# Two blocks of a transformer on one core: the score matmuls of two heads issued as one unit, in the two halves of the array's rows

## The chip, the cores and the metric

The kernel runs on one core of a Trainium2 chip. The metric is the device time of one execution in microseconds (us). Before the change it is 2282.53 us, the median of three runs (2281.49 to 2285.62).

## The reference, cut to what matters

The program has two blocks on 256 tokens of width 1024: a first block of two layers (mixers with three branches, a dense feed-forward, a mixture of experts), and a second block with two attention layers, called fox and dsw. Three pieces of it are attentions with heads of 64 channels, and they alone are touched. In short:

```python
# A: differential attention, one branch of the mixer, in both layers; 4 heads, two maps (m) each
s = einsum('bhmqd,bhmkd->bhmqk', qb, k)
s = where(mask, s - slopes * dist, -inf)
p = softmax(s); a = p[:, :, 0] - lam * p[:, :, 1]

# fox: 16 heads, causal, with a running sum c of log gates
s = einsum('bqhd,bkhd->bhqk', qi, k) * scale + ci[..., None] - c_k[:, :, None, :]
o = softmax(where(mask, s, -inf)) @ v

# dsw: 16 heads, three groups of dilated windows, softmax joined over the groups
s = einsum('znqhd,znkhd->znhqk', qb, band(kb)) * scale
```

All of it is float32, and the score products are float32 matmuls with 64 rows of contraction (the channels of a head).

## The kernel before, in words

Every engine call goes through a recorder (class `Recorder`, line 57). `add` (line 85) notes an operation with its engine, its tiles, its predecessors and an estimated cost, and `flush` (line 151) puts all operations of the program in order: a list scheduler that lets five engines run on its cost table, gives each engine the ready operation of highest priority, and hands out tiles of a tag strictly in the order in which they were asked for. The resulting order is then issued, and each engine runs its part in that order. All recorded instructions therefore carry one line number, L88, that of the closure in `add`.

PSUM has 8 banks: 3 with the tag `pa` (projections), 4 with `pb` (attention and other small work), 1 with `pt`. A bank counts as one region, whatever part of it is used.

Weights arrive as float32 (`raw`, on the queue of SP), ACT rounds them to a high part (`wh`), DVE subtracts to get the low part (`wl`), and TensorE multiplies in three passes with the activations' own two parts (`hh`, `hl`). This is most of TensorE's work. The attentions are woven between such projections.

An attention works on pairs of heads. The channels of the pair's first head lie in partitions 0 to 63 of the transposed queries and keys, those of the second in 64 to 127. For each head `e` of the pair a unit goes as follows: scores into one `pb` bank `p`; DVE masks them and finds the maxima; ACT takes exponentials into a tile `E2`; TensorE transposes the result into another `pb` bank; ACT copies that to SBUF; TensorE multiplies with the values into a third `pb` bank `o`, which the pair's units share.

- `a_heads` (line 1190): per pair 2 heads by 2 query blocks `b`; in each unit two maps `m`, each with a score matmul and then a bf16 matmul that adds the bias (identity times `biasA`).
- `fox`, its inner `attend` (line 1572): per pair 2 units; in each 4 bf16 matmuls that add the gates' sums, then score matmuls of 128 and of 256 columns. `attend(0)` is woven with projections, `attend(1)` with the first part of the output projection (`out_early`).
- `dsw`, its inner `attend` (line 1771): per pair 2 heads by 2 query blocks; in each unit three score matmuls, of 256, 128 and 128 columns, one per group. The four `attend` are woven with the next quarter's projections, the last one with `out_early`.

A float32 matmul leaves two records of a weight load and two of a matmul in the trace, of the same shape. There are 160 score matmuls: 32 in A, 32 in fox, 96 in dsw.

Of the kernel before, what the change touches and what calls it, by code (L numbers as in the profile page):

```python
# [4 lines left out]

# [1 line left out]

# [34 lines left out]
SWITCH, WAIT, URGENT, LOOK, RELEASE, TICK = 3000.0, 100.0, 20.0, 300.0, 1000.0, 10240 / 3  # L42
# [6 lines left out]


class Op:
    __slots__ = ("eng", "fn", "tiles", "dur", "table", "preds", "succs", "left", "ready", "prio", "bytes", "cols", "bias", "wait", "at", "name")


ENGINES = {"tensor": "PE", "vector": "DVE", "scalar": "ACT", "gpsimd": "POOL", "sync": "SP"}
# [3 lines left out]
class Recorder:  # L59
# [7 lines left out]
            setattr(s, name, Queue(s, name))  # L67

    def reset(s):
        s.ops, s.hist, s.bias, s.wait = [], {}, 0.0, WAIT  # L70

    def region(s, ap):

# [8 lines left out]
        ext = sum(abs(k) * (c - 1) for k, c in list(ap.ap)[1:]) + 1  # L82
        return t, p, p + n, f * size, (f + ext) * size

    def add(s, engine, method, args, kw):
        op = Op()
        op.eng, op.bias, op.wait = ENGINES[engine], s.bias, s.wait
        op.fn = lambda: getattr(getattr(s.nc, engine), method)(*args, **kw)  # L88
        aps = [x for x in args[1:] if hasattr(x, "tensor")] + [
            x for k, x in kw.items() if hasattr(x, "tensor") and k != "accum_out"]  # L90
        outs = [args[0]] + ([kw["accum_out"]] if kw.get("accum_out") is not None else [])
        s.cost(op, method, args, kw, outs[0], aps)
        op.name = method, outs[0].tensor.name, [z.tensor.name for z in aps]
# [3 lines left out]
        i = len(s.ops)  # L97
        preds = set()
        hit = lambda a, b: a[1] < b[2] and b[1] < a[2] and a[3] < b[4] and b[3] < a[4]
        for r in rd:  # L100
            ws, rs = s.hist.setdefault(r[0], ([], []))
            preds.update(j for q, j in ws if hit(q, r))
            if s.tag_of[r[0]] in BANKS:
                preds.update(j for q, j in rs if s.ops[j].eng != op.eng)
            rs.append((r, i))
        for r in wr:
            ws, rs = s.hist.setdefault(r[0], ([], []))
            preds.update(j for q, j in ws if hit(q, r))
            preds.update(j for q, j in rs if j != i and hit(q, r))
            inside = lambda q: r[1] <= q[1] and q[2] <= r[2] and r[3] <= q[3] and q[4] <= r[4]  # L110
            ws[:] = [z for z in ws if not inside(z[0])] + [(r, i)]
            rs[:] = [z for z in rs if z[1] == i or not inside(z[0])]
        op.preds = preds
        s.ops.append(op)

# [213 lines left out]
class Net:  # L329
# [860 lines left out]
    def a_heads(s, hp, qT, kT, va, neglam, sub, ya):  # L1190
        nc = s.nc
        o = s.ps("pb", (128, 4, 128))
        for e in range(2):
            h = 2 * hp + e
            ro = slice(e * 64, e * 64 + 64)
            for b in range(2):
                nk = 128 * (b + 1)
                p = s.ps("pb", (128, 2, 256))
                for m in range(2):
                    nc.tensor.matmul(p[:, m, 0:nk], qT[ro, 2 * m + hp, b * 128:b * 128 + 128],  # L1200
                                     kT[ro, 2 * m + hp, 0:nk], start=True, stop=False)
                    nc.tensor.matmul(p[:, m, 0:nk], s.identb, s.biasA[:, h, 256 - nk:256], start=False, stop=True)
                mx, sm = s.t([128, 2], "sa"), s.t([128, 2], "sa")
                nc.vector.tensor_reduce(mx, p[:, :, 0:nk], AX.X, ALU.max, negate=True)
                ex = s.t([128, 2, 256], "E2")
# [11 lines left out]
                at = s.t([128, 256], "E2")  # L1217
# [287 lines left out]
    def fox(s):  # L1505
# [66 lines left out]
        def attend(hf, T, v):  # L1572
            zh, zl = zs[hf]
            for pr in range(4):
                o = s.ps("pb", (128, 2, 2, 65))
                for e in range(2):
                    h = hf * 8 + pr * 2 + e
                    ro = slice(64 * e, 64 * e + 64)
                    q, k = T[0][ro, pr], T[1][ro, pr]
                    p = s.ps("pb", (128, 384))  # L1580
# [150 lines left out]
    def dsw(s):  # L1731
# [39 lines left out]
        def attend(qt, T, V):  # L1771

            z = zs[qt]
            for pr in range(2):
                o = s.ps("pb", (128, 2, 2, 65))
                for e in range(2):
                    ro = slice(64 * e, 64 * e + 64)
                    q, k = [T[g][ro, pr] for g in range(3)], [T[g][ro, 2 + pr] for g in range(3)]
                    vh = lambda g, kb: V[g][:, kb, pr * 2 + e]
                    for b in range(2):  # L1780
                        sl = slice(b * 128, b * 128 + 128)
# [8 lines left out]
                        for i, v in enumerate((vh(0, 0), vh(0, 1), vh(1, b), vh(2, b))):  # L1790
# [99 lines left out]
```

## Time and profile before

| what | us |
|---|---|
| median of three runs | 2282.53 |
| profiled execution, its own time | 2282.9 |
| its span, first to last instruction | 2280.9 |
| PE busy (matmul) | 2187.4 |
| DVE busy | 1733.8 |
| ACT busy | 1370.1 |
| attention A, layer 0 (stretch of the span) | 240 to 292 |
| attention A, layer 1 | 768 to 822 |
| attention fox | 1786 to 1896 |
| attention dsw | 1990 to 2264 |

PE is the matmuls of TensorE, PEld its weight loads, which overlap matmuls; DVE is VectorE, ACT ScalarE, POOL GpSimd, SP SyncE. Matmuls are pipelined, so a record is longer than the time from one start to the next: costs are read from start to start. A name such as `pb<-F,F` is the output's tile and the operands' tiles, with buffer numbers left out: `F`, `M`, `macc`, `g` hold transposed queries and keys in the attentions, `P` values, `E` softmax results, `T` and `G` other small tiles; a single operand name means that both operands lie in one tile. "64\*128" are the rows and columns of the array that a matmul uses.

### The profile page before, as it was taken

What the parts mean: (1) busy time and instruction counts of PE and PEld (TensorE: products, weight loads), DVE (VectorE), ACT (ScalarE), POOL (GpSimd) and SP (SyncE); (2) the same over time, 40 slices, a digit from 0 to 9 for tenths busy, and PEclk for the clock granted to TensorE, in tenths of its full rate; (3) what the DMA queues carried; (4) which work ended last, traced back from release to release, by engine and by line L of the source; (5) the groups of instructions that cost most, each with busy time, mean ns of one, the idle gap of its engine ahead of it and who ended that gap; (6) DMA issues with size and microseconds to landing.
All of it is one profiled execution on the core that took longest, in us unless ns stands there. A gap on an engine that the chain in (4) does not pass through costs nothing. (4 is left out here: it accounts for less than half of the span.)

```text
span 2280.9 us, 34038 instructions
## 1 busy us (share of the span) xinstructions
PE 2187.4 (96%) x13022; PEld 1884.2 (83%) x13022; DVE 1733.8 (76%) x2691; ACT 1370.1 (60%) x1915; POOL 173.0 (8%) x254
## 2 busy tenths in 40 slices
PE   4999999999999998999999999999997999999999
PEld 3888997998888897887888788778786777999997
DVE  7788778885789866888889888889886545655553
ACT  3664454344764445877777777777775545555553
POOL 3010001000020000000000000000002101322120
PEclk9999999999999997999999999999999999999999
DMA  8446656985436645799989999998985322534340
GB/s 318 173 142 236 210 202 222 340 297 180 171 121 213 215 164 185 257 331 352 350 307 373 332 350 331 369 340 305 363 302 204 130 74 93 167 122 134 125 139 19
DMA packets 281672, 527.95 MB, mean 231 GB/s; under 512 B 10362, under 2 KB 65872, under 8 KB 281504
## 3 DMA queue, kind: packets, MB, share of 16 engines
q1 hardware_dynamic: 279296, 522.23, 64.9%
q0 software_dynamic: 1696, 2.37, 0.3%
q8 instruction: 104, 1.70, 0.3%
q10 hardware_dynamic: 512, 1.13, 0.1%
q14 instruction: 64, 0.52, 0.1%
HBM read 524.64 MB, written 1.05 MB: 230 GB/s over the span
## 5 line engine op out<-in xcount | busy, mean ns | idle before, releaser
L88 DVE TENSOR_TENSOR wl<-raw,wh 128x1024 fp32r<-128x1024 f32 (+1 forms) x800 | 934.6, 1185 | 268.5 <-ACT wh L88 262.7
L88 ACT ACTIVATE wh<-raw 128x1024 fp32r<-128x1024 f32 (+1 forms) x800 | 810.9, 1031 | 455.2 <-PE pa L88 268.3
L88 PE MATMUL pa<-hh,wh 128*128 128x256 f32 x1072 | 303.1, 287 | 0.0
L88 PE MATMUL pa<-wh,hh 128*128 128x256 f32 (+1 forms) x920 | 297.8, 334 | 4.0 <-DVE P L88 1.7
L88 PE MATMUL pa<-hl,wh 128*128 128x256 f32 (+1 forms) x1072 | 299.8, 285 | 0.0
L88 PE MATMUL pa<-wl,hh 128*128 128x256 f32 (+1 forms) x920 | 297.2, 332 | 0.7 <-DVE wl L88 0.7
L88 PE MATMUL pa<-wh,hl 128*128 128x256 f32 (+1 forms) x920 | 297.1, 332 | 0.2 <-DVE hl L88 0.2
L88 PE MATMUL pa<-hh,wl 128*128 128x256 f32 x1056 | 297.2, 285 | 0.0
L88 PE MATMUL pa<-wh,Y 128*128 128x512 f32 (+1 forms) x784 | 248.5, 385 | 1.9 <-ACT Y L88 1.4
L88 PEld LDWEIGHTS pa<-hl,wh 128*128 128x128 f32 (+1 forms) x1072 | 202.8, 191 | 2.9 <-issue 2.5
L88 PEld LDWEIGHTS pa<-hh,wh 128*128 128x128 f32 x1072 | 203.4, 191 | 1.8 <-issue 1.4
L88 PEld LDWEIGHTS pa<-hh,wl 128*128 128x128 f32 x1056 | 200.8, 191 | 0.6 <-issue 0.3
L88 PEld LDWEIGHTS pa<-wh,hh 128*128 128x128 f32 x920 | 174.5, 193 | 20.9 <-issue 3.7
L88 PEld LDWEIGHTS pa<-wh,hl 128*128 128x128 f32 x920 | 174.7, 193 | 14.7 <-DVE hl L88 1.1
L88 PEld LDWEIGHTS pa<-wl,hh 128*128 128x128 f32 x920 | 174.6, 192 | 13.2 <-DVE wl L88 1.3
L88 PE MATMUL pb<-wh,P 128*128 128x512 f32 x544 | 181.8, 397 | 1.6 <-ACT P L88 1.4
L88 PEld LDWEIGHTS pa<-wh,Y 128*128 128x128 f32 x784 | 143.9, 189 | 32.3 <-ACT Y L88 2.5
L88 PE MATMUL pa<-wl,Y 128*128 128x512 f32 (+1 forms) x392 | 148.7, 383 | 0.2
L88 PE MATMUL pa<-wh,F 128*128 128x512 f32 (+1 forms) x376 | 137.3, 378 | 1.1 <-ACT wh L88 1.1
L88 DVE TENSOR_TENSOR M<-raw,M 128x1024 fp32r<-128x1024 f32 (+1 forms) x109 | 129.0, 1183 | 11.0 <-ACT M L88 10.6
L88 PE MATMUL pa<-wl,F 128*128 128x512 f32 (+1 forms) x344 | 129.3, 380 | 0.4
L88 ACT ACTIVATE T<-pa 128x256 f32<-128x256 f32 (+1 forms) x215 | 97.9, 488 | 45.7 <-PE pa L88 39.5
(372 smaller groups left out, 3683.0 us busy)
## 6 DMA issues: line engine op xcount, KB each, us to landing
raw<-in_moe_w SPq DMA_DIRECT2D x230, 1024.0 KB, 7.2
raw<-in_w_in SPq DMA_DIRECT2D x68, 1024.0 KB, 4.9
raw<-in_w_mod SPq DMA_DIRECT2D x36, 1024.0 KB, 5.4
raw<-in_dsw_w_in SPq DMA_DIRECT2D x72, 512.0 KB, 3.5
raw<-in_ffn_w SPq DMA_DIRECT2D x30, 1024.0 KB, 7.3
raw<-in_moe_w SPq DMA_DIRECT2D x48, 512.0 KB, 4.1
raw<-in_fox_w_in SPq DMA_DIRECT2D x16, 1024.0 KB, 6.0
raw<-in_w_mod SPq DMA_DIRECT2D x24, 512.0 KB, 5.1
```

The source lines that it names most:

```text
L88: op.fn = lambda: getattr(getattr(s.nc, engine), method)(*args, **kw)
```

## The change

The recorder gets a context `join`: all operations recorded inside become one operation for the scheduler, which issues them back to back. Its cost is that of the first plus half that of each further one. The two heads' units of a pair and query block now ask for their two `pb` banks together, and their score matmuls, alternating between the heads, are one joined operation. In A the bias comes first, one bf16 matmul per head for both maps (the bias is read twice by a broadcast), and the scores are added to it. In fox the bf16 matmuls of both heads come first. The softmax of the two heads and all that follows it is recorded head after head as it was.

```diff
+    @contextmanager
+    def join(s):
+        s.joined = []
+        yield
+        s.joined = None
...
+        first = s.joined
+        if first is not None and not first:
+            op.fns = [op.fn]
+            op.fn = lambda: [f() for f in op.fns]
+            first.append(op)
+        first = first[0] if first else None
...
+        if first is not None and first is not op:
+            preds.discard(i)
+            first.preds |= preds
+            first.tiles = sorted(set(first.tiles) | set(op.tiles))
+            first.fns.append(op.fn)
+            first.dur += op.dur * 0.5
+            first.cols += op.cols
+            return
...
     def a_heads(s, hp, qT, kT, va, neglam, sub, ya):
...
-                p = s.ps("pb", (128, 2, 256))
-                for m in range(2):
-                    nc.tensor.matmul(p[:, m, 0:nk], qT[ro, 2 * m + hp, b * 128:b * 128 + 128],
-                                     kT[ro, 2 * m + hp, 0:nk], start=True, stop=False)
-                    nc.tensor.matmul(p[:, m, 0:nk], s.identb, s.biasA[:, h, 256 - nk:256], start=False, stop=True)
+            ps = [s.ps("pb", (128, 2, 256)) for _ in range(2)]
+            for e, p in enumerate(ps):
+                bias = s.biasA[:, 2 * hp + e:2 * hp + e + 1, 256 - nk:256]
+                nc.tensor.matmul(p[:, :, 0:nk], s.identb, bias.to_broadcast([128, 2, nk]), start=True, stop=False)
+
+            with s.rec.join():
+                for m in range(2):
+                    for e, p in enumerate(ps):
+                        ro = slice(e * 64, e * 64 + 64)
+                        nc.tensor.matmul(p[:, m, 0:nk], qT[ro, 2 * m + hp, b * 128:b * 128 + 128],
+                                         kT[ro, 2 * m + hp, 0:nk], start=False, stop=m == 1)
...
-                    nc.tensor.matmul(p[:, 0:128], q[:, 0:128], k[:, 0:128], start=False, stop=False)
-                    nc.tensor.matmul(p[:, 128:384], q[:, 128:256], k, start=False, stop=True)
+                with s.rec.join():
+                    for (q, k), p in zip(qk, ps):
+                        nc.tensor.matmul(p[:, 0:128], q[:, 0:128], k[:, 0:128], start=False, stop=False)
+                    for (q, k), p in zip(qk, ps):
+                        nc.tensor.matmul(p[:, 128:384], q[:, 128:256], k, start=False, stop=True)
...
-                        p = s.ps("pb")
-                        nc.tensor.matmul(p[:, 0:256], q[0][:, sl], k[0], start=True, stop=True)
-                        for g in (1, 2):
-                            nc.tensor.matmul(p[:, 128 + g * 128:256 + g * 128], q[g][:, sl], k[g][:, sl],
-                                             start=True, stop=True)
+                    ps = [s.ps("pb") for _ in range(2)]
+
+                    with s.rec.join():
+                        for g in range(3):
+                            for e, p in enumerate(ps):
+                                if g == 0:
+                                    nc.tensor.matmul(p[:, 0:256], q[e][0][:, sl], k[e][0], start=True, stop=True)
+                                else:
+                                    nc.tensor.matmul(p[:, 128 + g * 128:256 + g * 128], q[e][g][:, sl], k[e][g][:, sl],
+                                                     start=True, stop=True)
```

The scheduler decides what this does to the order. On SP and POOL the instructions stand in the same order as before. On PE, DVE and ACT the order differs only in and around the attentions. Two places on PE show it.

The first is attention A of layer 1, the first unit of the second pair's first query block. `pb_1459` is the score bank of the first head, `F` are the queries and keys, `G_41_104` is the bias, `identb` the bf16 identity, `pa_1453` a projection. Before:

```order
L88 MATMUL pa_1453<-Y_1037_1100,wh_1454 128x256
L88 MATMUL pb_1452<-ident_67,E_1386_1449 128x128 x2
L88 MATMUL pb_1459<-F_1138_1201,F_1108_1171 128x128
L88 LDWEIGHTS identb_68
L88 MATMUL pb_1459<-G_41_104,identb_68 128x128
L88 MATMUL pb_1459<-F_1138_1201,F_1108_1171 128x128
L88 LDWEIGHTS identb_68
L88 MATMUL pb_1459<-G_41_104,identb_68 128x128
L88 MATMUL pa_1453<-Y_1038_1101,wh_1454 128x256
```

And with the change, at the same place, where `pb_1460` is the second head's bank:

```order
L95 MATMUL pb_1452<-ident_67,E_1386_1449 128x128 x2
L95 LDWEIGHTS identb_68
L95 MATMUL pb_1459<-G_41_104,identb_68 128x2x128
L95 LDWEIGHTS identb_68
L95 MATMUL pb_1460<-G_41_104,identb_68 128x2x128
L95 MATMUL pb_1459<-F_1138_1201,F_1108_1171 128x128
L95 MATMUL pb_1460<-F_1138_1201,F_1108_1171 128x128
L95 MATMUL pb_1459<-F_1138_1201,F_1108_1171 128x128
L95 MATMUL pb_1460<-F_1138_1201,F_1108_1171 128x128
L95 MATMUL pa_1453<-Y_1038_1101,wh_1454 128x256
```

Four score matmuls of 64 rows now stand in a row, where each stood alone between matmuls of 128 rows; the bias is one matmul per head in place of two.

The second is dsw, the second unit of the first pair, where the scheduler had put other matmuls between a unit's three score matmuls. `pt` is a transpose for a projection, `pb_24549` the output `o`. Before:

```order
L88 MATMUL pa_24563<-wh_24566,hh_24308 128x256
L88 MATMUL pb_24549<-P_5889_24397,E_6046_24554 128x65
L88 MATMUL pb_24555<-F_5842_24350 128x256
L88 MATMUL pt_24548<-ident_67,T_6034_24542 128x128
L88 MATMUL pb_24555<-F_5896_24404 128x128
L88 MATMUL pt_24548<-ident_67,T_6034_24542 128x128
L88 MATMUL pb_24555<-M_5950_24458 128x128
L88 MATMUL pb_24549<-P_5889_24397,E_6046_24554 128x65
```

And with the change, the joined unit of the pair's second query block:

```order
L95 MATMUL pa_24570<-wh_24571,hl_24293 128x256
L95 MATMUL pb_24575<-F_5842_24334 128x256
L95 MATMUL pb_24576<-F_5842_24334 128x256
L95 MATMUL pb_24575<-F_5896_24388 128x128
L95 MATMUL pb_24576<-F_5896_24388 128x128
L95 MATMUL pb_24575<-M_5950_24442 128x128
L95 MATMUL pb_24576<-M_5950_24442 128x128
L95 MATMUL pt_24565<-ident_67,T_6067_24559 128x128 x2
```

Six score matmuls follow each other, first head and second head in turn. Counted over the whole order of PE, the 160 score matmuls stood in 101 unbroken runs (32 in A, 16 in fox, 53 in dsw), and stand in 32 with the change (8, 8 and 16).

## Rows read from the trace of the kernel before

**Rows 1.** The page, busy time of each engine and its share of the span.

```profile
PE 2187.4 (96%) x13022; PEld 1884.2 (83%) x13022; DVE 1733.8 (76%) x2691; ACT 1370.1 (60%) x1915; POOL 173.0 (8%) x254
```

**Rows 2.** Stretches of A, fox, dsw: length, busy by engine, clock, DMA share, GB/s.

```profile
240.00:292.00 52.00, 51.62 (x384) 45.75 (x384) 41.66 (x68) 23.90 (x54) 1.70 (x2) 1.00 0.58 203
...
1786.00:1896.00 110.00, 106.29 (x613) 82.74 (x612) 52.92 (x126) 52.95 (x93) 10.16 (x10) 0.98 0.27 91
...
1990.00:2264.00 274.00, 272.80 (x2047) 251.02 (x2048) 151.32 (x370) 152.09 (x256) 48.70 (x76) 1.00 0.35 112
```

**Rows 3.** What PE waited for, 1786 to 1896: total us, times, longest.

```profile
PE pb L88 <- ACT E L88: 0.2, 1, 0.2
```

**Rows 4.** Matmuls by tile: duration ns min/median/max, starts, forms; the five 64-row groups.

```profile
L88 PE MATMUL pb<-F,F x96: 272/375/480, 240.0 to 1851.1; 64*128 64x128 f32 x48, 64*128 64x256 f32 x48
L88 PE MATMUL pb<-F x96: 269/376/480, 1989.8 to 2260.8; 64*128 64x256 f32 x64, 64*128 64x128 f32 x32
...
L88 PE MATMUL pb<-M x64: 272/272/373, 1990.6 to 2261.4; 64*128 64x128 f32 x64
...
L88 PE MATMUL pb<-g,macc x32: 272/375/378, 1857.3 to 1893.8; 64*128 64x128 f32 x16, 64*128 64x256 f32 x16
L88 PE MATMUL pb<-macc x32: 269/272/373, 2068.5 to 2261.1; 64*128 64x128 f32 x32
```

**Rows 5.** PE in time (start us, us): a whole dsw unit between projections.

```profile
1989.52 0.28 PE L88 MATMUL pa<-wl,hh 128*128 128x256 f32 x1
1989.64 0.28 PE L88 MATMUL pa<-wh,hl 128*128 128x256 f32 x1
1989.85 0.92 PE L88 MATMUL pb<-F 64*128 64x256 f32 x4
1990.60 0.38 PE L88 MATMUL pb<-M 64*128 64x128 f32 x2
1990.92 0.38 PE L88 MATMUL pa<-wh,hh 128*128 128x256 f32 x1
1991.14 0.28 PE L88 MATMUL pa<-wl,hh 128*128 128x256 f32 x1
```

**Rows 6.** PE in time: a dsw unit with transposes between its scores.

```profile
1996.43 0.70 PE L88 MATMUL pb<-F 64*128 64x256 f32 x2
1997.05 0.33 PE L88 MATMUL pt<-ident,T 128*128 128x128 f32 x1
1997.31 0.48 PE L88 MATMUL pb<-F 64*128 64x128 f32 x2
1997.73 0.33 PE L88 MATMUL pt<-ident,T 128*128 128x128 f32 x1
```

**Rows 7.** PE in time: a unit of A, layer 1.

```profile
785.33 0.48 PE L88 MATMUL pb<-F,F 64*128 64x128 f32 x2
785.75 0.23 PE L88 MATMUL pb<-G,identb 128*128 128x128 bf16 x1
785.91 0.48 PE L88 MATMUL pb<-F,F 64*128 64x128 f32 x2
```

**Rows 8.** PE in time: products with values, 65 columns wide.

```profile
2239.41 1.11 PE L88 MATMUL pb<-P,E 128*128 128x65 f32 x8
2240.32 0.48 PE L88 MATMUL pa<-wh,Y 128*128 128x512 f32 x1
```

**Rows 9.** PE in time: the last unit of fox and what follows.

```profile
1892.86 0.49 PE L88 MATMUL pb<-M,M 96*128 96x384 bf16 x4
1893.28 0.92 PE L88 MATMUL pb<-g,macc 64*128 64x128 f32 x4
1894.13 0.66 PE L88 MATMUL pb<-P,E 128*128 128x65 f32 x4
...
1900.95 1.22 PE L88 MATMUL pa<-wh,Y 128*128 128x512 f32 x2 [1.41 <-ACT Y L88]
```

**Rows 10.** ACT in time: one copy of transposed exponentials out of a `pb` bank, dsw.

```profile
2262.20 0.60 ACT L88 ACTIVATE E<-pb 128x512 f32<-128x512 f32 x1 [2.05 <-PE pb L88]
```

More of the change, by code (lines that the diff above doesn't have):

```diff
@@ L3 @@
 import math
-from contextlib import ExitStack
+from contextlib import ExitStack, contextmanager
 import numpy as np
@@ L51 @@
 class Op:
-    __slots__ = ("eng", "fn", "tiles", "dur", "table", "preds", "succs", "left", "ready", "prio", "bytes", "cols", "bias", "wait", "at", "name")
+    __slots__ = ("eng", "fn", "tiles", "dur", "table", "preds", "succs", "left", "ready", "prio", "bytes", "cols", "bias", "wait", "at", "name", "fns")
 ENGINES = {"tensor": "PE", "vector": "DVE", "scalar": "ACT", "gpsimd": "POOL", "sync": "SP"}
@@ L69, in reset @@
     def reset(s):
-        s.ops, s.hist, s.bias, s.wait = [], {}, 0.0, WAIT
+        s.ops, s.hist, s.bias, s.wait, s.joined = [], {}, 0.0, WAIT, None
     def region(s, ap):
@@ L96, in add @@
         op.tiles = sorted({r[0] for r in rd + wr})
-        i = len(s.ops)
+        first = s.joined
[4 more added lines that the diff above has]
+        first = first[0] if first else None
+        i = len(s.ops) - (first is not None and first is not op)
         preds = set()
@@ L112, in add @@
             rs[:] = [z for z in rs if z[1] == i or not inside(z[0])]
+        if first is not None and first is not op:
[6 more added lines that the diff above has]
+            return
+        preds.discard(i)
         op.preds = preds
@@ L1192, in a_heads @@
         o = s.ps("pb", (128, 4, 128))
[L1193 to L1197, printed above, removed]
-                p = s.ps("pb", (128, 2, 256))
-                for m in range(2):
-                    nc.tensor.matmul(p[:, m, 0:nk], qT[ro, 2 * m + hp, b * 128:b * 128 + 128],
-                                     kT[ro, 2 * m + hp, 0:nk], start=True, stop=False)
-                    nc.tensor.matmul(p[:, m, 0:nk], s.identb, s.biasA[:, h, 256 - nk:256], start=False, stop=True)
+        for b in range(2):
+            nk = 128 * (b + 1)
+            ps = [s.ps("pb", (128, 2, 256)) for _ in range(2)]
[3 more added lines that the diff above has]
+            with s.rec.join():
+                for m in range(2):
+                    for e, p in enumerate(ps):
[3 more added lines that the diff above has]
+            for e, p in enumerate(ps):
+                h = 2 * hp + e
                 mx, sm = s.t([128, 2], "sa"), s.t([128, 2], "sa")
@@ L1575, in attend @@
                 o = s.ps("pb", (128, 2, 2, 65))
-                for e in range(2):
+                ps = [s.ps("pb", (128, 384)) for _ in range(2)]
+                for e, p in enumerate(ps):
                     h = hf * 8 + pr * 2 + e
-                    ro = slice(64 * e, 64 * e + 64)
-                    q, k = T[0][ro, pr], T[1][ro, pr]
-                    p = s.ps("pb", (128, 384))
                     nc.tensor.matmul(p, sel[:, h], cp, start=True, stop=False)
@@ L1584, in attend @@
                                          sel[:, h], start=False, stop=False)
-                    nc.tensor.matmul(p[:, 0:128], q[:, 0:128], k[:, 0:128], start=False, stop=False)
-                    nc.tensor.matmul(p[:, 128:384], q[:, 128:256], k, start=False, stop=True)
+                qk = [[T[i][64 * e:64 * e + 64, pr] for i in range(2)] for e in range(2)]
+                with s.rec.join():
[3 more added lines that the diff above has]
+                        nc.tensor.matmul(p[:, 128:384], q[:, 128:256], k, start=False, stop=True)
+                for e, p in enumerate(ps):
                     ex = s.t([128, 384], "E2")
@@ L1775, in attend @@
                 o = s.ps("pb", (128, 2, 2, 65))
[L1776 to L1781, printed above, removed]
-                        p = s.ps("pb")
-                        nc.tensor.matmul(p[:, 0:256], q[0][:, sl], k[0], start=True, stop=True)
-                        for g in (1, 2):
-                            nc.tensor.matmul(p[:, 128 + g * 128:256 + g * 128], q[g][:, sl], k[g][:, sl],
-                                             start=True, stop=True)
+                q, k = ([[T[g][64 * e:64 * e + 64, i + pr] for g in range(3)] for e in range(2)] for i in (0, 2))
+                vh = lambda g, kb, e: V[g][:, kb, pr * 2 + e]
+                for b in range(2):
+                    sl = slice(b * 128, b * 128 + 128)
+                    ps = [s.ps("pb") for _ in range(2)]
+                    with s.rec.join():
+                        for g in range(3):
+                            for e, p in enumerate(ps):
+                                if g == 0:
[3 more added lines that the diff above has]
+                                                     start=True, stop=True)
+                    for e, p in enumerate(ps):
                         ex = s.t([128, 512], "E2")
@@ L1789, in attend @@
                         t = s.flip(ex, 4)
-                        for i, v in enumerate((vh(0, 0), vh(0, 1), vh(1, b), vh(2, b))):
+                        for i, v in enumerate((vh(0, 0, e), vh(0, 1, e), vh(1, b, e), vh(2, b, e))):
                             nc.tensor.matmul(o[:, b, e], t[:, i], v, start=i == 0, stop=i == 3)
```

## The prediction

> **What bounds the kernel now.** I read the shares of the engines first: PE is busy 96% of the span, DVE 76%, ACT 60% [rows 1]. A share is a mean over stages, so next come the stretches that the change touches. There PE leaves almost nothing: 51.62 of 52 us in A of layer 0, 106.29 of 110 in fox, 272.80 of 274 in dsw; DVE is at 41.66, 52.92 and 151.32 in them, and TensorE's granted clock is 0.98 to 1.00, its 2.4 GHz level [rows 2]. The waits say the same from the other side: in fox PE waited once, 0.2 us, for an exponential [rows 3]. So in these stretches the order of PE is full, the softmax runs beside projections, and what PE no longer has to do comes off the time, as long as the next matmul in its order is ready. The change takes away no arithmetic of weight. It changes which matmuls stand next to each other.
>
> **What a score matmul costs.** I use starts, since a record's length includes its drain. The 64-row records are 192 of 128 columns and 128 of 256 columns, 320 for 160 matmuls [rows 4]. Call b and a the time of one such record and c what a run of them adds between its first start and the next instruction's start. In the unit that is broken up, two records of 256 take 1997.05 - 1996.43 = 0.62 = c + 2a, two of 128 take 1997.73 - 1997.31 = 0.42 = c + 2b [rows 6]. The whole unit takes 1990.92 - 1989.85 = 1.07 = c + 2a + 4b [rows 5]. So b = 0.1125, a = 0.2125, c = 0.195 us. Fox agrees: 1894.13 - 1893.28 = 0.85 for two of each leaves 0.20 [rows 9]. All scores together are 128 x 0.2125 + 192 x 0.1125 = 27.2 + 21.6 = 48.8 us.
>
> **What a run costs besides.** Between 128-row and 64-row matmuls PE pauses on both sides. From transpose to transpose it is 1997.73 - 1997.05 = 0.68, less two records (0.225) and a transpose at the 0.11 of other 128-column float32 work: 0.345 [rows 6]. From projection to projection it is 1991.14 - 1989.64 = 1.50, less two slots of 0.12 and 2a + 4b = 0.875: 0.385 [rows 5]. In A it is 785.91 - 785.33 = 0.58, less 0.225 and 0.05 for 128 bf16 columns at the granted clock: 0.305 [rows 7]. In fox it is c = 0.20 and, ahead, 1893.28 - 1892.86 = 0.42 less 768 bf16 columns (0.32), 0.10: 0.30 [rows 9].
>
> **The change part by part.**
>
> *Fewer runs.* The order has 101 runs before and 32 after: 24 fewer in A, 8 in fox, 37 in dsw. 24 x 0.305 + 8 x 0.30 + 37 x 0.365 (mean of the two dsw prices) = 7.3 + 2.4 + 13.5 = **23.2 us less**. With 0.30 for all it is 20.7, with 0.385 for all 26.6. This needs nothing but that a run of both heads pays like a run of one.
>
> *The bias of A.* 16 bias matmuls in place of 32, with the same columns. One takes about 0.05 us of columns and some start-up; I take 0.05 each, **0.8 us less**, between 0 and 1.6.
>
> *Two halves side by side.* In the trace the two heads' scores never follow each other, so whether a matmul of rows 0 to 63 runs beside one of rows 64 to 127 is not shown, and neither is a price for going from one half to the other. The bound at no overlap is 0. The bound at full overlap is half of 48.8, 24.4, less about 0.1 us at the start of each of 32 runs, where nothing stands beside the first record: 21 us. What lies between is set by the weight loads: each record has one, and it is the 128 columns of the load that take time, not the rows. The products with values show it: with 65 columns the eight records still take 2240.32 - 2239.41 = 0.91, 0.114 each [rows 8], as much as a 64-row record of 128 columns. If loads follow each other at 0.11, the 128-column records gain nothing, and the 256-column ones go from 0.2125 to the load's 0.11: 128 x 0.10 = 13 us, less 0.1 at the start of the 28 runs that hold them: **10 us less**. I take this, since it is the value nearest to a row; ends 0 and 21. What would cost time here stands among the rivals. The Trainium skill says more (TensorEngine Tiling, Key Properties): tiles of the array are independent, and different tiles can load weights and multiply in parallel. By that rule loads would not queue either, and the whole would be 11 us shorter than my sum.
>
> *New waits.* A joined unit needs two of the four `pb` banks at once; `o` holds one, the transposes of the unit before another. The first head's softmax also starts later, after scores of both, and the second head's comes behind it on DVE and ACT. Where projections fill the order this is covered: PE hardly waits for an exponential as it is [rows 3], and ACT is busy 152 of 274 us in dsw [rows 2]. It is not covered at the end of fox, where PE already stood 1.41 us until ACT had the last piece, 6.8 us after the last scores (1894.13 to 1900.95) [rows 9]; a second head's softmax in that chain adds about 1 us. In A of layer 0 DVE is busy 41.66 of 52 us [rows 2]; with PE 6 us shorter it would be 41.66 of 46, so a little of A's gain is lost to it. I add **2 us** for both, from 0 to 5. The queues of SP and POOL keep their order, and no DMA is moved past anything.
>
> **The sum.** -23.2 - 0.8 - 10 + 2 = -32.0. The profiled execution took 2282.9 us (span 2280.9 and 2.0 around it), so 2250.9; the median of the runs is 0.4 lower, so I predict **2250.5 us**.
>
> **The rivals.**
>
> *Only the runs.* The halves do not overlap at all: no record stands beside another, and a joined run takes as long as its records one after the other. For it: no row shows overlap, and every pair of neighbouring 64-row records in the trace goes one by one. Against it: those are all of one half. The sum is -22.0, 2260.5 us.
>
> *Full overlap, loads too.* Then the third term is 21: -43, 2239.5 us. For it speaks that a load of 64 rows leaves the other rows of the array alone; against it that no two loads in the trace start closer than what rows 8 give for this width.
>
> *Waits for banks take the overlap back.* PE comes to a joined unit before the second bank is free, since a bank is released only when ACT has copied the transposes out. Price: 0.60 us, one such copy [rows 10], for each of the 24 units of fox and dsw, 14 us: 2264.5. Against it: counted over the changed order, at least 20 rows of other matmuls stand between two joined units of dsw.
>
> *Slower: every change of half pauses like a change of rows.* If going from rows 0 to 63 to rows 64 to 127 drains the array as going from 128 rows to 64 does, each alternation pays. There are 3 in a unit of A and fox, 5 in dsw: 8 x 3 + 8 x 3 + 16 x 5 = 128. At A's 0.305 that is 39 us, against 22 gained: +17, 2299.5 us. It decides from 22 / 128 = 0.17 us per alternation on. For it: the pause is in every row where the row count changes. Against it: within a run the tile and the bank's columns change without any pause (0.1125 each). The Trainium skill (TensorEngine Tiling, Key Properties) has a rule on just this: a change of the tiling mode drains TensorE, a change of tile alone does not. By that rule, with whose first half the rows here agree, the chance of this rival is small.
>
> **How the numbers follow.** Forecast 0.38 (2250.5), full overlap 0.22 (2239.5), only the runs 0.25 (2260.5), waits for banks 0.08 (2264.5), pauses at each change of half 0.07 (2299.5). The range goes from 2237 to 2266: the outer two of the first four, with 2.5 and 1.5 us more for the bounds of the price of a run (20.7 to 26.6 against 23.2). It leaves out the last. A measurement of this kernel tells about 0.2%, 4.6 us, from no change. The first four are faster by far more: 0.93, of which I move 0.02 to no change and 0.01 to slower for what I have not thought of, so faster 0.90, same 0.02, slower 0.08.
>
> **What would show it.** Right, step by step: in the changed profile a dsw unit's six score matmuls in one stretch of PE, between projections, in about 1.4 us of slots plus 0.4 of pauses (without overlap 1.75 + 0.4, with full overlap 1.0 + 0.4); 64-row weight loads 0.11 us apart; the pause on either side as before; PE still busy nearly throughout fox and dsw, with no new wait over 1 us at a score or a transpose. The two stretches of A shorter by about 5 us each, fox by 4, dsw by 18, and everything between them unchanged. The forecast is wrong if 256-column scores still start 0.21 us apart (only the runs), if starts inside a unit are 0.2 us or more further apart than before (pauses), or if PE waits for ACT ahead of the units (banks).

## The result, and the profile after

| | us | ratio to before, 95% interval |
|---|---|---|
| before, median | 2282.53 | |
| changed, median of four runs (2228.31 to 2230.30) | 2229.18 | 0.9764, 0.9748 to 0.9781 |
| changed, profiled execution | 2230.3 (span 2228.4) | |
| predicted | 2250.5 (2237 to 2266) | |

A fourth execution of the kernel before took 5417.81 us and is left out of its median. The change makes the kernel 53.4 us faster, 2.4%. The direction and the bottleneck were predicted; the size was not: 32 us were expected, and the measured time lies below the range. The profiled executions differ by 2282.9 - 2230.3 = 52.6 us, and that is the sum to explain.

The shares of the engines hardly move, as [rows 1] had them. PE still fills the span; 53.7 us of its busy time are gone:

```profile
PE 2133.7 (96%) x13006; PEld 1851.6 (83%) x13006; DVE 1729.7 (78%) x2691; ACT 1366.8 (61%) x1915; POOL 175.2 (8%) x254
```

Where they went is read by stage. Six normalisations begin with the same transposes of PE in both kernels, so their starts part the span into stages that can be laid side by side. The columns are those of [rows 2]; the four stages are the mixer of layer 0, the mixer of layer 1, fox, and dsw to the end. Before:

```profile
30.70:355.00 324.30, 315.86 (x2104) 282.37 (x2104) 268.00 (x471) 173.92 (x274) 23.79 (x32) 1.00 0.58 206
...
564.20:882.80 318.60, 308.29 (x2062) 273.72 (x2062) 253.16 (x437) 180.40 (x282) 24.90 (x34) 1.00 0.52 181
...
1724.70:1907.60 182.90, 169.89 (x936) 135.36 (x937) 98.47 (x199) 96.18 (x157) 21.89 (x25) 0.96 0.39 134
1907.60:2280.80 373.20, 363.77 (x2720) 336.34 (x2720) 207.57 (x497) 201.36 (x347) 72.80 (x103) 0.99 0.37 118
```

After:

```profile
30.90:349.20 318.30, 309.45 (x2097) 279.42 (x2096) 266.99 (x470) 173.61 (x274) 24.75 (x32) 1.00 0.60 210
...
558.40:871.30 312.90, 302.46 (x2054) 271.10 (x2054) 252.49 (x437) 179.86 (x282) 25.26 (x34) 1.00 0.53 184
...
1713.10:1881.10 168.00, 157.55 (x936) 128.18 (x936) 97.83 (x199) 95.13 (x158) 21.00 (x25) 0.98 0.42 143
1881.10:2228.30 347.20, 335.49 (x2720) 318.27 (x2720) 205.65 (x497) 199.82 (x347) 74.05 (x103) 1.00 0.40 128
```

The two mixers lose 6.0 and 5.7 us (about 5 each was expected), fox 14.9 (4 was expected), dsw and the end 26.0 (18 was expected). The two stages without attention, the feed-forward and the mixture of experts, stay within 0.1 us. So the gain is where the change is, and fox and dsw hold the surprise.

What happens inside is plain in one joined unit of dsw, PE in order of time (columns as in [rows 5]). It is the same kind of unit as in [rows 5], with the scores of both heads:

```profile
1962.23 0.28 PE L95 MATMUL pa<-wh,hl 128*128 128x256 f32 x1
1962.44 0.92 PE L95 MATMUL pb<-F 64*128 64x256 f32 x8
1963.20 0.39 PE L95 MATMUL pb<-M 64*128 64x128 f32 x4
1963.52 0.38 PE L95 MATMUL pa<-wh,hh 128*128 128x256 f32 x1
1963.74 0.28 PE L95 MATMUL pa<-wl,hh 128*128 128x256 f32 x1
```

Twelve 64-row records stand between the two projections. From the projection before them to the second one behind them it is 1963.74 - 1962.23 = 1.51 us. In [rows 5] the same distance, with six records, was 1.50. The second head's scores cost nothing. The weight loads of the unit tell why:

```profile
1962.44 0.73 PEld L95 LDWEIGHTS pb<-F 64*128 64x128 f32 x8
1963.09 0.31 PEld L95 LDWEIGHTS pb<-M 64*128 64x128 f32 x4
```

Twelve loads start within 1962.44 to 1963.21. They do not follow each other at 0.11 us, the pace of [rows 8]: they come in pairs, one of each half, which the trace has 6 to 7 ns apart (1962.443 and 1962.449, 1962.766 and 1962.773, and so on), and their matmuls likewise (1962.444 and 1962.451). Over all of dsw, fox and A the busy time of the 64-row records falls to less than half, from 85.1 to 39.7 us, the sums of their eight groups. Of these groups by line, operation and shape (columns: count, then busy us and mean ns of one, then idle time before), one of before and the same of after:

```profile
L88 PE MATMUL pb<-F 64*128 64x256 f32 x64 | 22.3, 428 | 0.0
```

```profile
L95 PE MATMUL pb<-F 64*128 64x256 f32 x64 | 11.2, 428 | 0.0
```

A record is as long as before (428 ns on the mean), and 64 of them fill half the time. From the starts of the whole trace, the time that goes to 64-row records and to the pauses around their runs is 48.4 us less: 24.3 from the overlap (e1 below against the change), the rest from the runs. It is counted run by run, from the start of the matmul ahead of a run to that of the second one behind it, less the slots that such matmuls take elsewhere. Some 4 us are left for something else; the experiments look for it in fox.

### The profile page after: what moved, and what is told of

Same layout as the page of the kernel before. It is cut to its first block, busy times and chain, and to the rows that moved or that the text cites. A ratio compares the mean times of both kernels' runs of the same rounds, so it can differ in the third digit from the quotient of the medians.

```text
span 2228.4 us, 34024 instructions
## 1 busy us (share of the span) xinstructions
PE 2133.7 (96%) x13006; PEld 1851.6 (83%) x13006; DVE 1729.7 (78%) x2691; ACT 1366.8 (61%) x1915; POOL 175.2 (8%) x254
## 5 line engine op out<-in xcount | busy, mean ns | idle before, releaser
L95 DVE TENSOR_TENSOR M<-raw,M 128x1024 fp32r<-128x1024 f32 (+1 forms) x109 | 128.8, 1182 | 11.8 <-ACT M L95 11.3
```

## The experiments

All times are medians of four or five runs, with runs of the kernel before on the same chip beside them; the ratio is to those. The medians of the kernel before were 2281.2 for e1 to e4, 2283.2 for e5 to e8 and 2281.7 for f1 and f2, so differences of under 2 us between these groups mean nothing. Where a stage is given, it is cut as above, from one execution; fox in the change and in e2, where its scores overlap as fully, differs by 1.9 us.

| kernel | us | ratio, 95% interval | fox | dsw to end |
|---|---|---|---|---|
| before | 2282.53 | | 182.9 | 373.2 |
| the change | 2229.18 | 0.9764, 0.9748 to 0.9781 | 168.0 | 347.2 |
| e1, both heads in the same half | 2252.39 | 0.9876, 0.9860 to 0.9893 | 172.5 | 359.7 |
| e2, head by head | 2238.27 | 0.9808, 0.9792 to 0.9825 | 169.9 | 354.8 |
| e3, fox as before | 2242.78 | 0.9830, 0.9813 to 0.9846 | 181.6 | 348.0 |
| e4, fox alone | 2266.92 | 0.9937, 0.9921 to 0.9954 | 168.4 | 372.0 |
| e5, not joined | 2262.62 | 0.9905, 0.9888 to 0.9921 | 175.5 | 361.2 |
| e6, full cost in the planner | 2234.40 | 0.9782, 0.9766 to 0.9798 | 170.0 | 351.4 |
| e7, two by two | 2229.28 | 0.9765, 0.9748 to 0.9781 | 168.3 | 347.3 |
| e8, four banks | 2226.07 | 0.9745, 0.9729 to 0.9762 | 168.5 | 344.7 |
| f1, the change again | 2230.37 | 0.9773, 0.9759 to 0.9786 | | |
| f2, four banks again | 2227.14 | 0.9758, 0.9745 to 0.9772 | | |

The theory after the result: 101 runs became 32, and in those the two halves of the array work side by side in full, loads included. The first rival: the overlap is small, and the order around the units explains the rest.

**e1, both heads in the same half of the rows.** The order of PE is that of the change, matmul by matmul; only the half of the rows of the second head's scores is another. The kernel leaves out the second head's scores and computes the first head's twice.

```diff
-                        ro = slice(e * 64, e * 64 + 64)
+                        ro = slice(0, 64)
...
-                qk = [[T[i][64 * e:64 * e + 64, pr] for i in range(2)] for e in range(2)]
+                qk = [[T[i][0:64, pr] for i in range(2)] for e in range(2)]
...
-                q, k = ([[T[g][64 * e:64 * e + 64, i + pr] for g in range(3)] for e in range(2)] for i in (0, 2))
+                q, k = ([[T[g][0:64, i + pr] for g in range(3)] for e in range(2)] for i in (0, 2))
```

> The changed kernel in the same order, but both heads' scores read the first head's queries and keys, so all of them use rows 0 to 63 (the second head's scores are left out and the first's computed twice). Theory now: the halves run fully side by side, matmuls and weight loads, which is worth half of the 48.6 us of score records, 24.3 us. Then this kernel takes 2229 + 24 = 2253 us, with six dsw matmuls of a joined unit in 1.75 us of slots, and fox from its norm to the next norm takes 168 + 5 = 173 us. Rival: the gain beyond fewer runs comes from the new order and fewer waits, not from overlap: then it stays near 2230 to 2235, and fox near 168.

Measured 2252.39, as the theory has it. A dsw unit, in the rows of PE:

```profile
2130.82 0.28 PE L95 MATMUL pa<-wh,hl 128*128 128x256 f32 x1
2131.03 1.57 PE L95 MATMUL pb<-F 64*128 64x256 f32 x8
2132.44 0.61 PE L95 MATMUL pb<-M 64*128 64x128 f32 x4
2132.98 0.39 PE L95 MATMUL pa<-wh,hh 128*128 128x256 f32 x1
2133.20 0.28 PE L95 MATMUL pa<-wl,hh 128*128 128x256 f32 x1
```

The distance is 2133.20 - 2130.82 = 2.38 us against 1.51 in the change, so 0.87 more, the 0.875 that one head's scores were worked out to be in the prediction. This one edit parts the gain: 2282.5 to 2252.4 is what fewer runs (and the order) give, 2252.4 to 2229.2, 23 us, is the two halves side by side (25.6 by the two ratios, 24.3 by the starts). From the starts, the pauses of this kernel's 32 runs come to 11.4 us; before they were 35.5 in 101. That is 0.36 and 0.35 a run: a run with the scores of two heads pays what a run of one paid.

**e2, the scores head by head.** The joined unit stays, but all matmuls of the first head come before those of the second, in place of turn by turn.

```diff
             with s.rec.join():
-                for m in range(2):
-                    for e, p in enumerate(ps):
+                for e, p in enumerate(ps):
+                    for m in range(2):
...
                     for (q, k), p in zip(qk, ps):
                         nc.tensor.matmul(p[:, 0:128], q[:, 0:128], k[:, 0:128], start=False, stop=False)
-                    for (q, k), p in zip(qk, ps):
                         nc.tensor.matmul(p[:, 128:384], q[:, 128:256], k, start=False, stop=True)
...
                     with s.rec.join():
-                        for g in range(3):
-                            for e, p in enumerate(ps):
+                        for e, p in enumerate(ps):
+                            for g in range(3):
```

> Joined units as in the change, each head in its own half, but all scores of the first head ahead of those of the second. Theory: matmuls start in order, so only the last of the first head and the first of the second stand side by side: 0.2 us saved in each of 32 units against no overlap, 2253 - 6 = 2247 us. Rival: TensorE's queue finds the other half's work further back, and order inside the unit does not matter: 2229 us.

Measured 2238.27, which neither had. In A and fox, where a head has two matmuls (four records), the overlap is still full. In dsw, with three matmuls (six records) a head, it is partial:

```profile
2122.30 0.28 PE L95 MATMUL pa<-wh,hl 128*128 128x256 f32 x1
2122.51 1.02 PE L95 MATMUL pb<-F 64*128 64x256 f32 x5
2123.27 0.27 PE L95 MATMUL pb<-M 64*128 64x128 f32 x1
2123.38 0.38 PE L95 MATMUL pb<-F 64*128 64x256 f32 x1
2123.38 0.27 PE L95 MATMUL pb<-M 64*128 64x128 f32 x1
2123.59 0.38 PE L95 MATMUL pb<-F 64*128 64x128 f32 x2
2123.81 0.38 PE L95 MATMUL pb<-M 64*128 64x128 f32 x2
2124.12 0.39 PE L95 MATMUL pa<-wh,hh 128*128 128x256 f32 x1
2124.35 0.28 PE L95 MATMUL pa<-wl,hh 128*128 128x256 f32 x1
```

The distance is 2124.35 - 2122.30 = 2.05 us, 0.54 over the change's; times 16 units, 8.6 us, and 9.1 were lost (7.6 of them in the stage of dsw). The group of five records in the second row holds four of the first head and one of the second: their starts in the trace are 2122.513, 2122.833, 2123.049, 2123.055 and 2123.158, and the fourth of these, 6 ns behind its neighbour, is the second head's first, the seventh in the order. It ran beside the third. The distance of 0.54 us from the unit's first start is the same in all 16 units, of which five have a wait on that load and eleven have none, so a wait is not what held it. So the order in which the halves are issued does matter, and the seventh could begin four places early, not six.

**e3 and e4, parts of the change.** e3 has the change in A and dsw, and fox as it was; e4 has it in fox alone. The edits are those of the change itself, put back in the other functions.

```diff
-                ps = [s.ps("pb", (128, 384)) for _ in range(2)]
-                for e, p in enumerate(ps):
+                for e in range(2):
...
+                    p = s.ps("pb", (128, 384))
...
-                with s.rec.join():
...
+                    nc.tensor.matmul(p[:, 0:128], q[:, 0:128], k[:, 0:128], start=False, stop=False)
+                    nc.tensor.matmul(p[:, 128:384], q[:, 128:256], k, start=False, stop=True)
```

> The change in A and dsw alone. If the stages add up, fox's share of 14.9 us (182.9 to 168.0 between norms) is missing: 2229 + 15 = 2244 us. If the part of it that the score matmuls do not explain (6 us of waits and of half clock) belongs to where fox falls in time and not to its own order, it is 2229 + 9 = 2238.

> The change in fox alone. If fox's 14.9 us is its own: 2282.5 - 15 = 2267.5 us, and the granted clock stays at 2.4 GHz through fox's end. If the 6 us not explained by its score matmuls come from elsewhere: 2282.5 - 9 = 2273.5 us, with stretches of 1.2 GHz as before the change.

Measured 2242.78 and 2266.92, both by the theory. The parts add up: in e4 fox takes 168.4 us and dsw 372.0, in e3 fox takes 181.6 and dsw 348.0. The 15 us of fox are its own, and not a consequence of what comes before it. But its 64-row records and pauses give only 8.7 of them. As the first case of e4's expectation had it, the granted clock is 1.00 in e4's last 7 us of fox. In e3 two waits of the kernel before are back (1.6 us for `sa`, 1.4 for `Y`; see e5), with 3.4 us at a granted clock of 0.50 from 1795.9 on.

**e5, not joined.** The two heads' scores are recorded turn by turn as in the change, but each is an operation of its own, so that the scheduler may put others between.

```diff
-            with s.rec.join():
+            if True:
...
-                with s.rec.join():
+                if True:
...
-                    with s.rec.join():
+                    if True:
```

> The change's code with the joins taken away: both banks asked together, bias first, scores recorded in turn, but each score matmul is an operation of its own, which the scheduler may part. Its order has 78 runs of scores in place of 32, nearly all of one head. Theory: 46 more runs at 0.365 us are 17 us, and the overlap's 24 us are gone: 2229 + 41 = 2270 us. Rival: overlap reaches across a few other matmuls, or the two banks and the bias are what matters: 2235 to 2250.

Measured 2262.62, less of a loss than the theory expected and more than the rival. The scheduler broke the 32 units into 78 runs. One of dsw:

```profile
1994.47 0.28 PE L95 MATMUL pa<-wh,hh 128*128 128x256 f32 x1
1994.68 0.70 PE L95 MATMUL pb<-F 64*128 64x256 f32 x2
1995.30 0.39 PE L95 MATMUL pa<-wl,hh 128*128 128x256 f32 x1
...
1995.97 0.48 PE L95 MATMUL pb<-F 64*128 64x128 f32 x2
1996.39 0.44 PE L95 MATMUL pt<-ident,T 128*128 128x128 f32 x2
```

Two records of 256 columns take 1995.30 - 1994.68 = 0.62 us from their first start to the next instruction's, as in [rows 6]. To record the scores turn by turn is worth little by itself: 33 us of the 53 need the join. The theory's 2270 was too much because it took nearly all runs to be of one head: 13 of dsw's 38 runs hold both, eight of them whole units. The scheduler put these head after head, and they overlap in part, as in e2: 1.61 us from the first start to the next instruction's in both.

Fox is the useful part. It has 16 runs here, none with any overlap, as before, and still takes 7.4 us less than before. That part of its gain comes with the order in which its work is now recorded: banks of both heads asked for together, and both heads' bf16 matmuls first. It shows in the waits and the clock. Before, PE stood for 1.65 us ahead of some transposes, and for 1.41 us at the end of the last attention until ACT had `Y` [rows 9]:

```profile
1807.77 0.63 PE L88 MATMUL pt<-ident,T 128*128 128x128 f32 x4 [1.65 <-DVE sa L88]
```

Close to the end of each of the two, the granted clock fell to half, 1.2 GHz, for 3.4 us (columns as above; the last but two is the granted clock):

```profile
1808.60:1812.00 3.40, 3.40 (x10) 2.63 (x9) 0.55 (x1) 1.57 (x2) 0.00 (x0) 0.50 0.28 107
1900.70:1904.10 3.40, 3.15 (x7) 2.48 (x8) 1.04 (x3) 0.20 (x1) 0.00 (x0) 0.50 0.62 188
```

The end of fox in the change:

```profile
1870.00:1884.00 14.00, 12.20 (x55) 8.83 (x53) 10.16 (x19) 8.76 (x18) 1.66 (x4) 1.00 0.38 117
```

The rows of PE's waits in fox, before and then after (columns: who waited for whom, us in total, times, longest):

```profile
PE pt L88 <- DVE sa L88: 1.7, 1, 1.7
PE pa L88 <- ACT Y L88: 1.4, 1, 1.4
```

```profile
PE pa L95 <- ACT wh L95: 1.0, 1, 1.0
PE pt L95 <- ACT wh L95: 0.7, 1, 0.7
```

The two waits of before are not among those of after, where a wait of 1.0 for ACT's `wh` (also there before) and a new one of 0.7 stand. By stage, PE's idle time in fox falls from 182.90 - 169.89 = 13.0 to 168.00 - 157.55 = 10.5 us, and its busy time by 12.3, of which 8.7 are scores and pauses, if the pauses are counted as busy. For the other 3.6 the clock is an explanation that has about the right size. In the two stretches at 0.50 PE is busy for 3.40 and 3.15 us, and a matmul of 512 columns takes 0.43 us from start to start there (1810.50 to 1810.93) against 0.23 behind them (1813.48 to 1813.71); half of 6.55 is 3.3 us, an estimate. Behind the first 14 us of its stage, fox has no stretch at 0.50 in any of the change, e1, e2, e4, e5, e7 and e8. e3, with fox as before, has one, and e6 has one (3.4 us from 1808.8 on, at a wait of 1.6). A wait of this length is not enough: the change has one of 1.6 at 1752.68, and the clock stays. That the waits lowered the clock was not tried by itself.

**e6, the planner's cost.** The join counts each further operation at half; here at its full cost. No matmul changes, only the order that the scheduler makes.

```diff
-            first.dur += op.dur * 0.5
+            first.dur += op.dur
```

> The change with one number altered: a joined operation costs the scheduler the full sum, not the first and half of each other. Scores run as in the change (32 runs, full overlap), about 1360 places of PE's order differ. Theory: the 6 us that fox gained beyond its score matmuls are waits and half clock that a given order has or has not. Then this kernel keeps 48 us for certain and may lose or keep those 6: 2229 to 2236 us, the difference in fox. Rival: they come with the shorter units whatever the order: 2229 us.

Measured 2234.40, some 5 us slower than the change, and than e7 on the same chip. The intervals of the ratios overlap (0.9766 to 0.9798, and 0.9748 to 0.9781 for both others); the single runs do not (2232.92 to 2237.62 against 2227.88 to 2231.32 in e7). The size is at the upper end of what the theory allowed, the place is another. Fox takes 170.0, which is as much as in e2 (169.9), and dsw 351.4 against 347.2. There PE is as busy as in the change (335.4 against 335.5 us) and stands for longer, above all at transposes that wait for `T` of DVE; from fox's end to the end of the kernel, the change and then e6:

```profile
PE pt L95 <- DVE T L95: 5.4, 9, 1.6
```

```profile
PE pt L95 <- DVE T L95: 8.8, 12, 1.7
```

So another order of the same matmuls costs about 5 us in this kernel, by waits of PE. It is one order; what orders differ by in general is not shown.

**e7, two by two.** To test what e2 had shown, dsw's scores go two of the first head, two of the second, and then one of each. If a record can start beside one up to four places ahead of it, this loses nothing; if the halves must alternate, or if a record with a wait of its own can't start early, it loses part of what e2 lost.

```diff
-                        for g in range(3):
-                            for e, p in enumerate(ps):
+                        for g, e in ((0, 0), (1, 0), (0, 1), (1, 1), (2, 0), (2, 1)):
+                            for p in ps[e:e + 1]:
```

> The change with dsw's six score matmuls in the order first head two, second head two, first head one, second head one. In the run with head after head, fox and A (two matmuls of a head, four records, ahead of the other head's) overlapped as fully as in turn, while dsw (three matmuls, six records ahead) lost 0.53 us a unit. Theory: a record starts beside another if it stands at most four records behind it. Then this order overlaps fully: 2229 us. Rival: it is the semaphore wait on the second head's first matmul, seen in dsw there, that held it, or any order but strict turns loses in dsw: 2233 to 2238 us.

Measured 2229.28, ratio 0.9765, the change's. The unit in PE's rows:

```profile
2114.75 0.28 PE L95 MATMUL pa<-wh,hl 128*128 128x256 f32 x1
2114.96 0.93 PE L95 MATMUL pb<-F 64*128 64x256 f32 x8
2115.72 0.40 PE L95 MATMUL pb<-M 64*128 64x128 f32 x4
2116.04 0.38 PE L95 MATMUL pa<-wh,hh 128*128 128x256 f32 x1
2116.26 0.28 PE L95 MATMUL pa<-wl,hh 128*128 128x256 f32 x1
```

The distance is 1.51 us again. The fifth record, the second head's first, starts 13 ns behind the first one, although its load has a wait of its own, as in e2. So four records ahead are no hindrance, and six are.

**e8, four banks.** If a run costs 0.36 us whatever it holds, both query blocks of a pair in dsw can share one: 12 scores in four `pb` banks, 8 runs fewer. The bank of the output `o` is asked for later, after the first transposes.

```diff
-                o = s.ps("pb", (128, 2, 2, 65))
...
+                ps = [[s.ps("pb") for _ in range(2)] for _ in range(2)]
...
-                for b in range(2):
-                    sl = slice(b * 128, b * 128 + 128)
-                    ps = [s.ps("pb") for _ in range(2)]
-
-                    with s.rec.join():
+                with s.rec.join():
+                    for b in range(2):
+                        sl = slice(b * 128, b * 128 + 128)
...
+                        if o is None:
+                            o = s.ps("pb", (128, 2, 2, 65))
```

> A version that goes on: in dsw both query blocks of a pair are one joined unit of twelve score matmuls in four banks, and the output bank is asked for after them. 8 runs fewer, 8 x 0.385 = 3.1 us: 2226 us if other matmuls cover the wait for banks as they do now. Rival: all four banks of the tag are taken by one unit, and PE waits for the softmax of its first head before it can transpose: slower than 2229, by up to 1 us a pair, 8 us: 2234.

Measured 2226.07. A unit in PE's rows, its first and last ones:

```profile
2033.40 0.28 PE L95 MATMUL pa<-wh,hl 128*128 128x256 f32 x1
2033.61 0.70 PE L95 MATMUL pb<-F 64*128 64x256 f32 x4
...
2035.24 0.39 PE L95 MATMUL pb<-M 64*128 64x128 f32 x4
2035.56 0.39 PE L95 MATMUL pa<-wh,hh 128*128 128x256 f32 x1
2035.78 0.28 PE L95 MATMUL pa<-wl,hh 128*128 128x256 f32 x1
```

It takes 2035.78 - 2033.40 = 2.38 us. Two units of the change, with the two projection slots of 0.12 that each distance holds counted once, take 2 x 1.51 - 0.24 = 2.78. The 0.40 saved, 8 times, is 3.2 us. As the difference to the change is small, both were run again on one chip.

> The changed kernel unaltered, on the same chip as the next, for a direct comparison: 2229 us, 0.9765 of the kernel before.

> The version with twelve score matmuls in four banks in dsw, again: 3 us less than the changed kernel on the same chip, 2226 us, if the 8 runs saved are the cause; the same 2229 us if the earlier difference was chance.

Measured 2230.37 for the change and 2227.14 for four banks. The difference is 3.1 and 3.2 us, by the expected size, but the intervals of the ratios overlap (0.9759 to 0.9786 and 0.9745 to 0.9772), so it is seen twice and not set apart. Four banks have the lowest medians of all kernels run here.

Not tried: both heads' scores in one bank, written from the two halves at once, which would save a bank per unit.

## Why the prediction was wrong in size, step by step

The sum of the prediction is laid beside what was measured, in the profiled executions (from starts, or from the stages):

| step of the prediction | predicted us | measured us |
|---|---|---|
| Fewer runs | -23.2 | -24.1 |
| The bias of A | -0.8 | about 0 |
| Two halves side by side | -10 | -24.3 |
| New waits | +2 | about -4 |
| sum | -32.0 | -52.6 |

**What bounds the kernel: right.** PE's order was full, and what PE no longer did came off the time. The 48.4 us of records and pauses are in the 52.6. In fox the order was less full than the prediction read it: it took the one wait for an exponential [rows 3], and in the same window PE also waited 1.9 us for `T` and 1.7 for `sa`, both of DVE.

**Fewer runs: right.** 69 runs fewer gave 24.1 us (35.5 in 101 runs, 11.4 in e1's 32). The condition was that a run of both heads pays like a run of one, and e1 shows it: 0.36 us a run against 0.35.

**The bias of A: too small to be seen.** The two mixers lose 11.7 us together, and A's runs and overlap from the starts account for 11.8. The price of a pause is no more exact than that.

**Two halves side by side: this is the step that failed.** The mechanism was named; its size was off by 14 us. The prediction put weight loads at one per 0.11 us, because it found no closer pace in the trace before [rows 8]. Those loads go to the same rows. In the change, loads of different halves start 6 to 7 ns apart. In e1, with the same order and all loads in one half, the twelve loads of a unit start within 2131.03 to 2132.66, 1.63 us, where those of the change start within 0.77:

```profile
2131.03 1.38 PEld L95 LDWEIGHTS pb<-F 64*128 64x128 f32 x8
2132.33 0.52 PEld L95 LDWEIGHTS pb<-M 64*128 64x128 f32 x4
```

So the pace belonged to the rows and was no bound on the loads of both halves together, and the row that the estimate was taken from could not tell the two apart. Nor is it right that no two loads of the trace before start closer: at 240.38 two of 128 rows, of a transpose and of the projection behind it, start 4 ns apart. The far end, -21, was wrong as well: it took off 0.1 us at the start of each of the 32 runs, where nothing was thought to stand beside the first record. The first records of both halves start together (1962.444 and 1962.451), so there is no such loss, and the bound at full overlap is the plain half, 24.4. Measured were 24.3. The Trainium skill had the answer (TensorEngine Tiling, Key Properties): different tiles can load weights and multiply in parallel. The trace agrees, as twelve loads start within 0.77 us, where one per 0.11 would need 11 x 0.11 = 1.2. The prediction set that rule below its nearest row, and the row did not speak about the case.

**New waits: the sign was wrong.** The place that was named, the end of fox, is where time was gained: the wait of 1.4 us for `Y` is not in the rows after. Fox gave 6 us beyond its scores (14.9 - 8.7). In A nothing was lost. Dsw gave back 1.9 (27.9 of scores and pauses against 26.0 of the stage), as PE's idle time there rose from 373.20 - 363.77 = 9.4 to 347.20 - 335.49 = 11.7 us, with the waits for `T` up from 3.5 to 5.4. One of these is new and 1.6 us long, at a transpose at 1903.70, ahead of the first joined unit; the prediction had expected no new one of over 1 us. Together it is -4. e3, e4 and e5 show that fox's part comes with the order in which fox is recorded and not with the array, and e6 that another order costs 5 us at the same work. So the term hangs on the order that the scheduler makes, and the rows before did not hold it; in hindsight, 0 with about 5 us on either side would have been an honest term.

**The rivals.** *Only the runs* is what e1 builds: it took 2252 us, where the prediction had 2260.5 (the difference is mostly the term of the new waits, whose sign was wrong). *Full overlap, loads too* was the right one; its 2239.5 was 10 us too high through the start loss (3.3), the waits (6.2) and the runs (0.9), less the bias (0.8). *Waits for banks* did not come: no PE wait in dsw or fox is for ACT's copies (those for ACT are for `wh`, 1.0 and 0.7 us in fox). *Slower: every change of half pauses* is excluded: 1.51 us with five changes of half within the unit, against 1.50 with none. The Trainium skill has another rule at the same place (TensorEngine Tiling, Key Properties), that a change of the mode drains the array and a change of tile alone does not. The trace agrees on both sides: 0.36 us a run, and 6 to 7 ns from one half to the other.

**The range.** It was cut at 2237, by the case of full overlap less 2.5 us. With the overlap's bound put at its plain half, which the rows gave (24.4), that case is 2282.5 - 23.2 - 0.8 - 24.4 = 2234.1, and with some 5 us for the order on either side, which only e6 has shown, and on the slower side, it reaches from 2229 to 2239.

## What to carry to other kernels

Where matmuls use only half of the array's rows, issue those of the two halves next to each other, in separate PSUM banks and as one unit that a scheduler can't part: here the second half was free, and each unbroken run cost 0.3 to 0.4 us, whatever it held. Count runs first, and then halve the columns. And do not take the pace of one resource as a bound for another that the trace has never shown at work: when no row shows the two halves together, the full gain, with nothing taken off, belongs in the range.

## What the hardware showed that was not expected

- Weight loads of the two halves start 6 to 7 ns apart (13 ns in dsw of e7 and in A and fox of e2), as do their matmuls, though loads of 64 rows of one half follow each other at about 0.11 us or more.
- The halves need not alternate. In e7 and in A and fox of e2 a record starts beside one four places ahead of it; in dsw of e2, where six stand ahead, it starts beside the third of them, again four places ahead. No run tried other distances.
- In e2 a matmul started ahead of earlier ones: the seventh at 2123.055, the fourth at 2123.158. The Trainium skill (TensorE: Matmul & The Clock Gate, The mechanism) says that matmuls start and end in the order of the program, without exception. The trace differs for starts in different halves, and the measurement decides.
